# Longer waits ahead of layer 1's table and state products, C matrices on POOL's queue, readout products in one burst

## The chip, the cores and the metric

The kernel runs on one core of one Trainium2 chip. The metric is the device time of one execution in microseconds (us). The names of the engines are those of the profile: PE is the tensor engine, PEld its weight loads, DVE the vector engine, ACT the scalar engine, POOL GpSimd, SP the engine that issues most of the DMAs.

## The reference

Two layers, 256 latent and 256 context tokens of width 1024. Layer 0 treats all 512 tokens, layer 1 only the latent ones (of the context it needs the S5 states alone).

```python
for l in range(DEPTH):
    ...
    hc = _modulate(xc, g_norm1[l], csh1, csc1)
    if l == DEPTH - 1:
        ctx_states = _s5_states(hc @ w_in[l][:, :W_BRANCH], *s5p, None)
    else:
        zc = hc @ w_in[l]
        ctx_states = _s5_states(zc[..., :W_BRANCH], *s5p, None)
        xc = xc + cga1 * _token_mixer(zc, ctx_states, p)
        xc = xc + cga2 * _sq_relu_mlp(_modulate(xc, g_norm2[l], csh2, csc2), mlp_w1[l], mlp_w2[l])
    ctx_final = _s5_final(ctx_states)
    h = _modulate(x, g_norm1[l], sh1, sc1)
    z = h @ w_in[l]
    lat_states = _s5_states(z[..., :W_BRANCH], *s5p, ctx_final)
    x = x + ga1 * _token_mixer(z, lat_states, p)
    x = x + ga2 * _sq_relu_mlp(_modulate(x, g_norm2[l], sh2, sc2), mlp_w1[l], mlp_w2[l])
return _rms_norm(x, g_final)
```

`_token_mixer` runs four branches (the S5 scan in two directions, a Fourier mixing, pooling, a convolution module), gates each with a sigmoid of its own part of z, projects and adds them. The change touches the S5 branch only: 16 groups of 16 channels, 64 complex states for each group and direction, h_t = a h_(t-1) + Bbar u_t, and y = Re(C h) + D u.

## The kernel before

All large products are float32, done as three products of two-part operands (`mm3`): a 128x128 tile of weights costs three matmuls, on 512 columns in layer 0 and 256 in layer 1. Below they are called main products. `Stream` brings the weights in blocks of 512 KB by SP's queue; ACT makes the high part of each and DVE the low part (tiles called `parts`).

One program writes all instructions out ahead of time. It walks through the main products, and after every three of them calls `pump()`, which may let background tasks write some of theirs in between. A task is a generator: `yield "w", x` holds it back until x us more of the tensor engine's modelled time have been written. So the order on each engine is fixed by these numbers; on the chip an engine works through its instructions in that order and waits at one whose input is late.

The S5 branch works on chunks of 8 tokens, so that only 32 chunk states are scanned for each half of the tokens. Its steps, all background tasks:

- `tables_b` makes the powers of a times Bbar, eight pieces: some arithmetic, four transposes on PE, a copy, a DMA to a scratch in DRAM (`scr_b`).
- `tables_c` makes C times the powers of a, eight pieces (u, k): it loads the C matrices of each u (`load`, from the input `in_s5c`), fills `BL` with zeros (the MEMSET) and then with Bbar (the TENSOR_SCALAR), multiplies C with the powers, multiplies `BL` with the result on PE (`products`, four products of 112 columns, for k=1 eight more), and stores the result (`scr_c`).
- In layer 0 these arithmetic steps have two buffers (nb = 2). Layer 1's tables are made on POOL beside layer 0's MLP, with one buffer of each kind (nb = 1): a piece's arithmetic can start only when the stores of the piece before it have left the buffer.
- `states` loads the S5 input by chunks from a scratch (`load_u`: `scan<-scr_z`, on POOL's queue) and multiplies it with the B tables: four groups of 16 products of 64 columns.
- `scan` runs on DVE and POOL.
- `readout` makes y: for each unit (h, g) eight products of the window `T` and then four groups of eight products of the states with the C tables, all into the same two PSUM banks, 128 columns each. Layer 0 has four units, layer 1 two. In the trace eight such products are 16 records, since float32 goes through PE twice.

Every operation goes through `Engine.call`, so in the trace nearly every line is L64.

Of the kernel before, what the change touches and what calls it, by code (L numbers as in the profile page):

```python
# [25 lines left out]
class Alloc:  # L26
    """A bump allocator over one SBUF region (words of a partition)."""
# [24 lines left out]
class Engine:  # L52
    """An engine that keeps a clock of what it has been given, against the tensor engine's."""
# [15 lines left out]
class Engines:  # L69
    """The engines of a core, each with its clock."""  # L70
# [34 lines left out]
class S5:  # L105
    """The bidirectional state-space scan, in chunks of 8 tokens.

    Tokens: 64 chunks (32 of the context, 32 of the latents), seg = stream.
    State rows: partition (gi, p) for group g = 2 q + gi, free (direction k, q).
    """  # L110
# [135 lines left out]
    def powers(self, E, base, W, plan):  # L246
        """base[.., d:d+n] = base[.., s:s+n] * base[.., m]."""
        na = base.shape[2]
        for d, s, m, n in plan:
            t1 = W[:, 0:2 * na * n].rearrange("p (r a i) -> p r a i", r=2, i=n)  # L250
            sh = [128, na, n]
            br = bc(base[:, 0, :, m:m + 1], sh)
            bi = bc(base[:, 1, :, m:m + 1], sh)
            o = base[:, :, :, d:d + n]
            x = base[:, :, :, s:s + n]
            E.tensor_tensor(t1[:, 0], x[:, 1], bi, op=MUL)
            E.tensor_tensor(t1[:, 1], x[:, 0], bi, op=MUL)
            E.tensor_tensor(o[:, 0], x[:, 0], br, op=MUL)
            E.tensor_tensor(o[:, 1], x[:, 1], br, op=MUL)
            E.tensor_tensor(o[:, 0], o[:, 0], t1[:, 0], op=SUB)  # L260
            E.tensor_tensor(o[:, 1], o[:, 1], t1[:, 1], op=ADD)
            yield

# [1 line left out]
    def tables_b(self, A, E):  # L265
        K, l = self.K, self.l
        nc = K.nc
# [16 lines left out]
        for i in range(8):  # L284
# [14 lines left out]
            if nb == 1:  # L299
                yield "w", 6.0  # L300
            if i >= nb - 1:
                products(i + 1 - nb)
            if nb == 1:
                yield "w", 4.0
# [6 lines left out]
    def tables_c(self, A, E):  # L311
# [12 lines left out]
        def load(u):  # L324
            nc.sync.dma_start(CCs[u % 2], K.I["s5c"][l][u])
# [38 lines left out]
        for u in range(4):  # L364
# [8 lines left out]
            for k in range(2):  # L373
# [13 lines left out]
                if nb == 1:  # L387
                    yield "w", 6.0
# [3 lines left out]
                if nb == 1:  # L392
                    yield "w", 4.0
# [7 lines left out]
    def store_u(self, t, ps):  # L401
        """ps: the projection of channel tile t, [128, 512 tokens] in PSUM."""
        K = self.K
        z = K.tmp()
        K.nc.scalar.activation(
            z.rearrange("p (s j) -> p j s", s=8), ps.rearrange("p (j s) -> p j s", s=8), AF.Copy)
        K.nc.scalar.dma_start(K.Z[self.l][t], z)
# [20 lines left out]
    def permute(self, i, raw, T):  # L428
        """The windows of the kernel with their columns in the order of the readout."""
        self.K.nc.scalar.activation(T[:, 1024 * i:1024 * i + 1024].rearrange("p (g c t) -> p g c t", g=8, c=16),  # L430
                                    raw[:, 1024 * i:1024 * i + 1024].rearrange("p (g t c) -> p g c t", g=8, c=16),
                                    AF.Copy)

# [7 lines left out]
    def begin(self):  # L441
        """Space, and the tables as far as there is space for them."""
# [14 lines left out]
    def states(self):  # L457
# [3 lines left out]
        yield "w", 5.87 + (0.0 if l else 2.0)  # L461
# [27 lines left out]
    def scan_tables(self, E):  # L489
        """Powers of a^8, for both parts of every state; in the place of bbar and rev."""  # L490
# [32 lines left out]
    def level(self, k, i, p0, step, n, g0=0):  # L523
        """Positions p0, p0 + step, .. += a^(8 2^i) times the one before by 2^i in the direction's order."""
# [25 lines left out]
    def scan(self):  # L550
        """The scan over chunks: sums over pairs, fours, eights, then over the eights in order, and back."""
# [18 lines left out]
        # over the groups of eight chunks, in the order of the scan  # L570
# [29 lines left out]
    def readout(self):  # L600
        """y: [channel, (half, stream, step, chunk)], in the place of the tables of the scan."""
# [12 lines left out]
        for h in range(2):  # L614
# [13 lines left out]
            for g in gs:  # L628
# [8 lines left out]
                yield "w", 1.5  # L637
                for j, (k, r) in enumerate(((0, 0), (0, 1), (1, 0), (1, 1))):
# [8 lines left out]
                    yield "w", 1.5  # L647
# [11 lines left out]
    def load_d(self):  # L659
        """The input of the scan by channels."""  # L660
# [4 lines left out]
class Stream:  # L665
    """The large weights, in the order of their use: loaded ahead, split into two float32r parts."""
# [10 lines left out]
    def lend(self, until, slots):  # L677
        """More space for the parts of the entries before one."""
# [50 lines left out]
    def release(self, key=None):  # L729
        """Gives back the space of an entry, or of the first that holds some."""  # L730
# [7 lines left out]
class Model:  # L738
# [55 lines left out]
    def pool(self, side, dtype=F32, **sizes):  # L794
        """Tiles on a side of the shared space, in the place of what was there."""
# [4 lines left out]
    def open_scan(self, l):  # L800
        """Space for the state-space branch (and in the first layer for the convolution)."""
# [6 lines left out]
    def open_parts(self, w):  # L808
        """The parts of the merged branches in the place of the last two branches' space."""
# [17 lines left out]
    def open_hidden(self, i, l):  # L827
        """Space for a half of the MLP's hidden features at a time."""
# [11 lines left out]
    def lend_y(self, l):  # L840
        """Space for weights that a mixer needs from its first branch's output on."""
# [14 lines left out]
    def hold(self, n):  # L856
        """Waits until n banks can be kept beyond a step and one is left."""
# [9 lines left out]
    def defer(self, f):  # L867
        """Work that waits for another engine, to be given to its own a little later."""
# [6 lines left out]
    def mm3(self, out, w, x, start, stop):  # L875
        """out += w^T x for w and x in two float32r parts."""
# [9 lines left out]
    def after(self, *cbs):  # L886
        """After the products of an output tile: what follows the tile before, the next weights, background."""
# [16 lines left out]
    def pump(self):  # L904
        """Background work, as long as its engines are not behind: a task's step yields nothing, a wait
        in the tensor engine's time, or the engines of its next steps."""
# [42 lines left out]
    def order(self, l):  # L949
        """The branches of a mixer: f the inputs of the Fourier branch, g a tile of gates, y a branch's  # L950
        output in two parts, q a tile of its projection; each with the branch and the tile."""
# [36 lines left out]
    def warm(self, n):  # L988
        """Products that keep the tensor engine's clock up while the first data comes; nothing reads them."""
# [9 lines left out]
    def mod_part(self):  # L999
        """Two of the eight row tiles of four column tiles of the first norm's modulation, both conditions."""  # L1000
# [13 lines left out]
    def mod_finish(self, m):  # L1014
        """Shift and scale of two tiles of features."""
# [10 lines left out]
    def mod_bias(self, l, m, c, raw):  # L1026
        """Four column tiles of the modulation from their products, and what the norms need of them."""
# [11 lines left out]
    def mods(self):  # L1039
        """The modulation's other column tiles, with the rows of the weights on the free axis."""  # L1040
# [39 lines left out]
    def mod_need(self, l, m):  # L1080
        """The modulation's column tiles before one."""
# [47 lines left out]
    def norm_sums(self, acc, n, width):  # L1129
        """1 / sqrt(column sums of acc / width + eps) as diagonal matrices of tokens."""  # L1130
# [10 lines left out]
    def norm_bcast(self, d, n):  # L1141
        """The diagonal on every partition, in PSUM."""
# [7 lines left out]
    def h_tiles(self, l, which, r, c0, n):  # L1150
        """h = x r g (1 + scale) + shift in two parts; yields the tiles of features, one product ahead."""
# [49 lines left out]
    def turn(self, l, part, keys, xh, xl, l2, which, order):  # L1201
        """The last four output tiles before a norm; the norm of one half runs beside the products of the other."""
# [49 lines left out]
    def turned(self, h, l2, which, order, group):  # L1252
        """The first group of products after the norm, for one half; the norm and h of the other."""
# [32 lines left out]
    def layer(self, l):  # L1286
# [5 lines left out]
        # first output tiles, by rows of the weights as h comes  # L1292
# [196 lines left out]
        # output projection  # L1489
# [19 lines left out]
        # MLP  # L1509
# [127 lines left out]
    def shift_columns(self):  # L1637
        """The second norm's shift as columns before those of the tokens, which go without it and the norm's factor."""
# [35 lines left out]
    def run(self):  # L1674
# [61 lines left out]
        # the last norm, on the way to rows of tokens  # L1736
# [28 lines left out]
class Branches:  # L1765
    """The pooling, Fourier and convolution branches of a layer; y: their output in float32."""
# [12 lines left out]
    def linear(self, w, x):  # L1779
        """w^T x for a [256, 256] matrix and x [128, 2 n]; yields the two tiles in PSUM."""  # L1780
# [8 lines left out]
    # pooling  # L1789
# [52 lines left out]
    # Fourier mixing  # L1842
# [36 lines left out]
    # convolution  # L1879
# [20 lines left out]
    def conv(self):  # L1900
# [12 lines left out]
        # layer norm over the channels  # L1913
# [45 lines left out]
class S5L:  # L1959
    """The state-space branch of a layer."""  # L1960
# [105 lines left out]
def _rows(a):  # L2066
    """[.., 128 k] vectors onto partitions: [.., 128, k]."""
# [70 lines left out]
```

## Time and profile before

| | |
|---|---|
| time, median of 3 runs | 1219.62 us (1215.27 to 1221.63) |
| span of the profiled execution | 1223.4 us |
| PE busy | 1169.3 us, 96% of the span |
| DVE busy | 977.2 us, 80% |
| ACT busy | 515.9 us, 42% |
| POOL busy | 277.2 us, 23% |
| moved by DMA | 211.49 MB |

The profile is of one execution; its span lies 0.3% above the median, and what lies around the span is not shown. A row of the timeline gives the start, the length, the engine, the line, the operation with the tile it writes and those it reads, the count, and in brackets the idle time ahead of it with what ended it.

### The profile page before, as it was taken

To read this page: it belongs to the slowest core of one execution; us is meant where nothing else is said; L and a number is where in the kernel's file an instruction comes from. 1 tells how busy PE (TensorE), PEld (TensorE's weight loads), DVE (VectorE), ACT (ScalarE), POOL (GpSimd) and SP (SyncE) were. 2 spreads that over 40 slices of the span, in tenths; PEclk is the share of its full clock that TensorE was granted. 3 is DMA by queue.
4 is the path that set the end of the run, shared out by engine and by line. 5 is a ranking of instruction groups with operands and counts; after the bars stand their busy time and mean duration, and the time that the engine had idled before them with its cause. 6 is when DMAs were issued, how large, how long until landed. Compare 5 with 4: busy or idle time off the path is not lost.

```text
span 1223.4 us, 20288 instructions
## 1 busy us (share of the span) xinstructions
PE 1169.3 (96%) x7770; PEld 1007.1 (82%) x7770; DVE 977.2 (80%) x1878; ACT 515.9 (42%) x872; POOL 277.2 (23%) x315
## 2 busy tenths in 40 slices
PE   7999996999999999999988989998999999999997
PEld 5777775776787988888876878897999999999997
DVE  6789999788799769999986884556898788867664
ACT  4534342333334465422421433335544455645443
POOL 0048754000000100176535462030530002000000
PEclk9999998999999999999998999999999999999999
DMA  9543522546464514466676765335444445555551
GB/s 375 216 134 125 167 84 94 181 163 203 134 209 161 180 34 149 138 194 219 198 254 230 267 212 206 121 121 160 168 159 163 162 155 198 186 186 189 179 186 52
DMA packets 66961, 211.49 MB, mean 173 GB/s; under 512 B 7984, under 2 KB 14128, under 8 KB 66864
## 3 DMA queue, kind: packets, MB, share of 16 engines
q1 hardware_dynamic: 56032, 184.10, 44.8%
q10 hardware_dynamic: 7696, 14.56, 3.2%
q0 software_dynamic: 3136, 11.54, 2.9%
q8 instruction: 61, 1.00, 0.3%
q14 instruction: 36, 0.29, 0.1%
HBM read 199.19 MB, written 10.98 MB: 172 GB/s over the span
## 4 chain that ended last, share of the span: by engine, by line
PE 55%; DVE 26%; issue 6%; DMA 5%; ACT 4%; POOL 3%; ACTq 0%; DVEq 0%; POOLq 0%; SPq 0%
PE bank L64 55%; DVE whole L64 9%; DVE parts L64 7%; DVE scan L64 5%; DVE mixer L64 2%; ACT parts L64 2%; DMA whole<-in_w_modt_dram 1%; ACT whole L64 1%; POOL whole L64 1%; POOL tables L64 1%; DMA scr_c<-tables 1%; DVE windows L64 1%; DMA whole<-in_w_dram 1%; POOL scan L64 1%; DMA whole<-in_w_br_dram 1%
## 5 line engine op out<-in xcount | busy, mean ns | idle before, releaser
L64 PE MATMUL bank<-parts 128*128 128x512 f32 (+2 forms) x4008 | 729.2, 339 | 17.7 <-DVE parts L64 14.5
L64 PEld LDWEIGHTS bank<-parts 128*128 128x128 f32 x4008 | 612.4, 190 | 107.5 <-DVE parts L64 20.2
L64 ACT ACTIVATE parts<-whole 128x1024 fp32r<-128x1024 f32 (+1 forms) x288 | 273.1, 959 | 150.7 <-PE bank L64 67.7
L64 DVE TENSOR_TENSOR parts<-whole,parts 128x1024 fp32r<-128x1024 f32 (+1 forms) x240 | 292.7, 1227 | 16.4 <-ACT parts L64 16.0
L64 PE MATMUL bank<-hidden,parts 128*128 128x256 f32 (+1 forms) x1440 | 253.9, 337 | 0.0
L64 PEld LDWEIGHTS bank<-hidden,parts 128*128 128x128 f32 x1440 | 219.6, 190 | 30.6 <-issue 0.5
L64 DVE SCALAR_TENSOR_TENSOR whole<-whole 128x1024 f32<-128x1024 f32 (+3 forms) x186 | 174.0, 937 | 18.8 <-DMA whole<-in_w_modt_dram 15.6
L64 POOL TENSOR_TENSOR whole<-whole 128x256 f32<-128x256 f32 (+1 forms) x69 | 53.2, 785 | 338.1 <-ACT whole L64 325.0
L64 DVE SCALAR_TENSOR_TENSOR whole<-bank,whole 128x256 f32<-128x256 f32 (+1 forms) x121 | 54.6, 475 | 67.5 <-PE bank L64 67.4
L64 ACT ACTIVATE whole<-whole 128x256 f32<-128x256 f32 (+2 forms) x139 | 48.7, 387 | 104.2 <-DVE whole L64 95.3
L64 ACT ACTIVATE whole<-bank 128x512 f32<-128x512 f32 (+2 forms) x69 | 35.5, 537 | 133.0 <-PE bank L64 92.6
L64 DVE TENSOR_TENSOR whole<-whole 128x256 f32<-128x256 f32 (+7 forms) x158 | 72.5, 464 | 18.8 <-ACT whole L64 16.4
L64 ACT ACTIVATE mixer<-bank 128x512 f32<-128x512 f32 (+1 forms) x84 | 40.7, 496 | 105.4 <-PE bank L64 99.2
L64 POOL TENSOR_TENSOR tables<-tables,whole 128x256 f32<-128x256 f32 x48 | 61.7, 1292 | 42.9 <-DMA scr_c<-tables 40.4
L64 DVE TENSOR_TENSOR hidden<-whole,hidden 128x512 fp32r<-128x512 f32 (+2 forms) x77 | 54.3, 709 | 9.4 <-ACT hidden L64 2.3
L64 ACT ACTIVATE hidden<-whole 128x512 fp32r<-128x512 f32 (+2 forms) x77 | 47.1, 615 | 8.1 <-PE bank L64 2.3
L64 ACT ACTIVATE tables<-bank 128x512 f32<-128x512 f32 (+2 forms) x20 | 8.4, 420 | 92.0 <-PE bank L64 91.7
L64 DVE SCALAR_TENSOR_TENSOR scan<-scan,whole 128x512 f32<-128x512 f32 (+1 forms) x64 | 47.0, 795 | 0.0
L64 POOL COPY whole<-whole 128x32 f32<-128x32 f32 x20 | 11.3, 599 | 150.0 <-DVE whole L64 150.0
L64 POOL TENSOR_TENSOR scan<-scan,whole 128x256 f32<-128x256 f32 (+3 forms) x50 | 41.3, 839 | 17.6 <-DVE scan L64 13.1
L64 DVE TENSOR_TENSOR scan<-scan,whole 128x256 f32<-128x256 f32 (+5 forms) x61 | 30.8, 531 | 13.4 <-ACT whole L64 12.5
L64 DVE TENSOR_TENSOR mixer<-bank,mixer 128x512 f32<-128x512 f32 (+1 forms) x56 | 31.6, 570 | 10.4 <-PE bank L64 9.8
(114 smaller groups left out, 904.9 us busy)
## 6 DMA issues: line engine op xcount, KB each, us to landing
whole<-in_w_dram SPq DMA_DIRECT2D x128, 512.0 KB, 4.3
whole<-in_w_in_dram SPq DMA_DIRECT2D x84, 512.0 KB, 4.2
whole<-in_w_modt_dram SPq DMA_DIRECT2D x77, 512.0 KB, 4.3
whole<-in_w_br_dram SPq DMA_DIRECT2D x16, 512.0 KB, 3.9
whole<-in_w_out_dram SPq DMA_DIRECT2D x16, 512.0 KB, 3.9
mixer<-in_w_mod_dram SPq DMA_DIRECT2D x8, 512.0 KB, 8.6
scan<-scr_b POOLq DMA_DIRECT2D x8, 512.0 KB, 5.7
scan<-in_w_mod_dram SPq DMA_DIRECT2D x6, 512.0 KB, 8.9
```

The costliest lines, as they stand in the source:

```text
L64: return f(out, *a, **k)
```

## The change

Five places. In layer 1's tables (nb == 1) the wait between a piece's arithmetic and its products grows from 6.0 to 8.0 us and the one behind the products shrinks from 4.0 to 2.0. Layer 1's C matrices are loaded by POOL's queue instead of SP's. The wait ahead of the state products grows from 5.87 to 10.5 us in layer 1 and from 7.87 to 8.5 in layer 0. In `readout` the waits between the five groups of a unit go, and one wait stays behind the last group. All docstrings and comments are removed too, which shifts line numbers by one (2137 lines become 2136).

```diff
@@ tables_b @@
             if nb == 1:
-                yield "w", 6.0
+                yield "w", 8.0
             if i >= nb - 1:
                 products(i + 1 - nb)
             if nb == 1:
-                yield "w", 4.0
+                yield "w", 2.0
@@ tables_c @@
         def load(u):
-            nc.sync.dma_start(CCs[u % 2], K.I["s5c"][l][u])
+            (nc.gpsimd if l else nc.sync).dma_start(CCs[u % 2], K.I["s5c"][l][u])
...
                 if nb == 1:
-                    yield "w", 6.0
+                    yield "w", 8.0
                 todo.append((u, k))
                 if len(todo) == nb:
                     products(*todo.pop(0))
                 if nb == 1:
-                    yield "w", 4.0
+                    yield "w", 2.0
@@ states @@
         self.load_u()
-        yield "w", 5.87 + (0.0 if l else 2.0)
+        yield "w", 10.5 if l else 8.5
@@ readout @@
-                yield "w", 1.5
                 for j, (k, r) in enumerate(((0, 0), (0, 1), (1, 0), (1, 1))):
                     for qq in range(4):
...
                             nc.tensor.matmul(py[gi][32 * qq:32 * qq + 32, 0:128],
                                              SB[k][ps, r, 4 * h + qq, g, k:k + 32], ca[ps, c:c + 128],
                                              start=False, stop=j == 3, tile_position=(64 * gi, 32 * qq))
-                    yield "w", 1.5
+                yield "w", 1.5
```

PE, the first product of layer 1's C tables (`tables 32x112`), which stands among layer 0's second MLP product (`hidden,parts`), before:

```order
L64 MATMUL bank_64<-hidden_3352,parts 128x512 x24
L64 MATMUL bank_65<-hidden_3352,parts 128x512 x24
L64 MATMUL bank_66<-hidden_3352,parts 128x512 x3
L64 MATMUL bank_68<-tables 32x112 x4
L64 MATMUL bank_66<-hidden_3352,parts 128x512 x21
L64 MATMUL bank_70<-hidden_3352,parts 128x512 x24
L64 MATMUL bank_63<-hidden_3352,parts 128x512 x6
L64 MATMUL bank_69<-tables 32x112 x4
```

and of the change:

```order
L64 MATMUL bank_64<-hidden_3352,parts 128x512 x24
L64 MATMUL bank_65<-hidden_3352,parts 128x512 x24
L64 MATMUL bank_66<-hidden_3352,parts 128x512 x12
L64 MATMUL bank_68<-tables 32x112 x4
L64 MATMUL bank_66<-hidden_3352,parts 128x512 x12
L64 MATMUL bank_70<-hidden_3352,parts 128x512 x24
L64 MATMUL bank_63<-hidden_3352,parts 128x512 x15
L64 MATMUL bank_69<-tables 32x112 x4
```

The product stands nine main products later; the 51 main products between one piece's products and the next are the same number as before.

POOL, the start of layer 1's C tables, before:

```order
L64 MEMSET tables 128x256
L64 TENSOR_SCALAR tables<-tables 128x64
L64 TENSOR_TENSOR tables<-tables,whole 128x256
L64 TENSOR_TENSOR whole<-tables,whole 128x256
L64 TENSOR_TENSOR tables<-tables,whole 128x256 x2
```

and of the change:

```order
L64 MEMSET tables 128x256
L64 DMA tables<-in_s5c_dram 128x128 x2
L64 TENSOR_SCALAR tables<-tables 128x64
L64 TENSOR_TENSOR tables<-tables,whole 128x256
L64 TENSOR_TENSOR whole<-tables,whole 128x256
```

The loads of the first two C matrices now stand in POOL's own order, right behind the MEMSET; each of the other two stands behind a piece with k=1 and ahead of the next TENSOR_SCALAR. Before, the four stood on SP among the weight loads.

PE, layer 1's state products (`scan 64x64`) among the input projection (`parts 128x256`), before:

```order
L64 MATMUL bank_66<-parts 128x256 x24
L64 MATMUL bank_70<-parts 128x256 x21
L64 MATMUL bank_68<-scan 64x64 x16
L64 MATMUL bank_70<-parts 128x256 x3
L64 MATMUL bank_63<-parts 128x256 x9
L64 MATMUL bank_69<-scan 64x64 x16
```

and of the change:

```order
L64 MATMUL bank_66<-parts 128x256 x24
L64 MATMUL bank_70<-parts 128x256 x24
L64 MATMUL bank_63<-parts 128x256 x24
L64 MATMUL bank_64<-parts 128x256 x15
L64 MATMUL bank_68<-scan 64x64 x16
L64 MATMUL bank_64<-parts 128x256 x3
```

The first group stands 42 main products later (3 + 24 + 15), and with it everything of the branch that follows.

## Rows read from the trace of the kernel before

**Rows 1.** The page, busy time of each engine, share of the span.

```profile
PE 1169.3 (96%) x7770; PEld 1007.1 (82%) x7770; DVE 977.2 (80%) x1878; ACT 515.9 (42%) x872; POOL 277.2 (23%) x315
```

**Rows 2.** Waits of PE: us in total, times, longest.

```profile
PE bank L64 <- POOL tables L64: 10.3, 5, 4.4
...
PE bank L64 <- issue: 3.9, 1, 3.9
```

**Rows 3.** Timeline of PE, first unit of layer 0's readout.

```profile
230.76 0.45 PE L64 MATMUL bank<-scan 64*32 64x128 f32 x16
231.14 2.35 PE L64 MATMUL bank<-parts 128*128 128x512 f32 x9
233.42 0.45 PE L64 MATMUL bank<-scan 64*32 64x128 f32 x16
```

**Rows 4.** Timeline of PE, main products behind a unit, then what follows.

```profile
311.37 19.36 PE L64 MATMUL bank<-parts 128*128 128x512 f32 x84
330.56 1.02 PE L64 MATMUL bank<-scan,whole 128*128 128x512 f32 x2
```

**Rows 5.** Timeline of PE cut off at 230.85: the first eight records alone.

```profile
230.76 0.34 PE L64 MATMUL bank<-scan 64*32 64x128 f32 x8
```

**Rows 6.** Timeline of PE, products of layer 1's C tables.

```profile
643.31 0.59 PE L64 MATMUL bank<-tables 128*32 128x112 f32 x4 [4.37 <-POOL tables L64]
646.17 0.59 PE L64 MATMUL bank<-tables 128*32 128x112 f32 x4 [2.28 <-POOL tables L64]
646.69 13.34 PE L64 MATMUL bank<-hidden,parts 128*128 128x512 f32 x51
...
726.31 0.39 PE L64 MATMUL bank<-tables 128*32 128x112 f32 x4 [1.69 <-POOL tables L64]
```

**Rows 7.** Timeline of POOL, layer 1's C tables.

```profile
624.66 0.31 POOL L64 MEMSET tables<- 128x256 f32 x1 [6.69 <-DMA scr_b<-tables]
638.38 1.04 POOL L64 TENSOR_SCALAR tables<-tables 128x64 f32<-128x64 f32 x1 [13.41 <-DMA tables<-in_s5c_dram]
...
644.53 1.59 POOL L64 TENSOR_TENSOR tables<-tables,whole 128x256 f32<-128x256 f32 x1
...
718.50 0.65 POOL L64 TENSOR_TENSOR tables<-tables,whole 128x256 f32<-128x256 f32 x1 [5.63 <-DMA scr_c<-tables]
```

**Rows 8.** Timeline of SP, the first two C loads.

```profile
633.40 0.86 SPq L325 DMA_DIRECT2D tables<-in_s5c_dram  x2
```

**Rows 9.** Loads from scr_z by POOL's queue, issue to landing.

```profile
DMA to landing us min/median/max: 4.1/5.4/7.9
```

**Rows 10.** Windows: us, busy PE, PEld, DVE, ACT, POOL, PEclk, DMA share, GB/s.

```profile
638.00:650.00 12.00, 5.35 (x22) 3.48 (x21) 10.97 (x16) 1.42 (x2) 7.58 (x7) 0.72 0.83 268
863.00:867.00 4.00, 4.00 (x75) 3.49 (x74) 2.82 (x8) 2.60 (x8) 0.53 (x1) 1.00 0.70 212
```

**Rows 11.** Timeline of PE, layer 1's state products.

```profile
846.11 5.42 PE L64 MATMUL bank<-parts 128*128 128x256 f32 x43 [0.49 <-DVE parts L64]
855.39 1.97 PE L64 MATMUL bank<-scan 128*64 128x64 f32 x32 [3.86 <-issue]
857.29 2.93 PE L64 MATMUL bank<-parts 128*128 128x256 f32 x12
860.15 1.49 PE L64 MATMUL bank<-scan 128*64 128x64 f32 x32
```

**Rows 12.** Timeline of POOL, layer 1's load of the S5 input.

```profile
847.26 1.18 POOL L64 DMA_DIRECT2D scan<-scr_z  x1 [27.38 <-DMA scr_z<-whole]
```

**Rows 13.** A window of layer 1, the columns of rows 10.

```profile
857.00:914.00 57.00, 55.08 (x481) 52.67 (x477) 53.09 (x131) 30.13 (x59) 28.36 (x35) 0.97 0.47 158
```

**Rows 14.** Timeline of PE, three waits on DVE and POOL.

```profile
208.85 1.65 PE L64 MATMUL bank<-parts 128*128 128x512 f32 x3 [9.53 <-DVE parts L64]
...
421.33 0.61 PE L64 MATMUL bank<-whole 128*128 128x1 f32 x4 [1.19 <-POOL whole L64]
...
914.02 0.38 PE L64 MATMUL bank<-parts 128*128 128x256 f32 x1 [1.11 <-DVE parts L64]
```

## The prediction, made before the changed kernel ran

> **What bounds the kernel now.** I read the page first. PE is busy 96% of the span and DVE 80% [rows 1], so nearly every microsecond has to come from PE: either it waits less, or it loses less between instructions, or it runs at its full clock for longer. So I next asked the view of waits what PE waits for. Of some 54 us idle, 10.3 us in five waits are for POOL's arithmetic on layer 1's tables, and one of 3.9 us is put down to "issue", which is a DMA here as shown below [rows 2]. Then I looked at the timeline of PE at each of the five places of the diff, and behind each at what comes next, since what PE no longer waits for here it may wait for there.
>
> **Readout bursts.** In the first unit of layer 0 a group of 16 records starts at 230.76, main products follow at 231.14, and the next group starts at 233.42 [rows 3]: 2.66 us for one group and nine main products. A main product costs (330.56 - 311.37) / 84 = 0.2285 us in a long run of them [rows 4], nine cost 2.06, so a group costs 0.60 us. How long would it take in a burst? The trace has no burst of several groups, but half a group shows the rate: the first eight records end at 230.76 + 0.34 = 231.10 [rows 5], all sixteen at 231.21 [rows 3], so eight more take 0.11 and sixteen 0.22. Each break of the main stream thus costs 0.60 - 0.22 = 0.38 us by itself. A unit breaks it five times before (the window's group and four others) and once after: 4 x 0.38 = 1.52 us, and 6 x 1.52 = 9.1 us for the six units. I take the same price for the 256-column products of layer 1. Lower bound: only the slow resumption of the main stream (0.60 less the 0.38 from 230.76 to 231.14, so 0.22) is saved, 6 x 4 x 0.22 = 5.3 us. The small products need no cover, since PE has none; what follows on ACT and DVE comes at nearly the same place, because the task waits 1.5 us behind the last group as before.
>
> The Trainium skill speaks against so short a group: by "TensorE: Matmul & The Clock Gate", section "Wait — 56ns, not 53.3ns?", matmuls start no closer than about 25 ns. Sixteen records would then take 0.40 us in a burst, and the bursts would save 4.8 us (an estimate from that page of the skill). The trace shows eight more records in 0.11 us, 14 ns each, which that rule does not allow, so the row decides.
>
> **Layer 1's tables.** PE reaches the first C product at 643.31 - 4.37 = 638.94, waits 4.37 us, and for its second half 2.28 more [rows 6]. What is late is POOL: it fills `BL` at 624.66, then idles 13.41 us for the C matrices until 638.38, and works until 644.53 + 1.59 = 646.12 [rows 7]. SP issues the two loads only at 633.40 [rows 8], between weight loads. From POOL's queue they can go out right behind the MEMSET. That one waits for the last B piece's store, whose product stands nine main products later now, 2.06 us, so the MEMSET ends at about 627.0. For the issue of two loads I take 1.2 us, that of the one in [rows 12], for the landing the median of POOL's loads from `scr_z`, 5.4 us [rows 9]: 633.6. POOL's work of 646.12 - 638.38 = 7.74 us ends at 641.4. PE comes nine main products later as well, at 641.0, so it waits 0.4 instead of 6.65: 6.25 us.
>
> With the wait goes a stretch at a lower clock. Between 638 and 650 the granted clock averages 0.72, a mixture of its two levels of 1.2 and 2.4 GHz, after PE was busy 5.35 of the 12 us [rows 10]; the 51 main products behind the wait take 13.34 us [rows 6] where 51 x 0.2285 = 11.65 would do. So 1.7 us more: 7.9 us in all. Lower bound: a landing of 7.9 us [rows 9] leaves 2.9 us of wait, and the low clock may stay: 6.65 - 2.9 = 3.7 us. The other waits for POOL's tables are 1.69 at 726.31 [rows 6] and 10.3 - 6.65 - 1.69 = 2.0. The loop behind them is products, store, POOL, products: POOL waits 5.63 us for the store [rows 7], and the store starts with the products. With 8.0 + 2.0 instead of 6.0 + 4.0 its period does not change, so I count nothing; upper bound both, 3.7 us, and the last 0.4.
>
> What is queued behind the moved loads? The third and fourth stand on POOL ahead of the next TENSOR_SCALAR, and wait there for a k=1 piece's products on PE, for which that instruction waits anyhow (one `BL`). They can cost their issue, at most 2 x 1.2 us, if POOL is the late one there; the pieces right behind them show no wait of PE, so I take nothing. SP loses a wait; no wait of PE is for a weight's DMA there, so this too is worth nothing.
>
> **State products.** In layer 1 the load of the S5 input is issued at 847.26 [rows 12], and PE waits from 851.53 until 855.39 [rows 11]: 8.1 us after the issue, so "issue" is this landing. A main product costs 5.42 / 43 = 0.126 us here, and 42 of them put PE's arrival at 856.8, after the landing: 3.86 us gained. The twelve main products behind the first two groups take 860.15 - 857.29 = 2.86 us [rows 11] where 1.51 would do, so 1.35 at the lower clock may come back: 5.2 us. But the branch now starts about as late as before in time and 42 products later in order, and DVE is busy 53.09 of the next 57 us [rows 13], with PE waiting 1.11 us for it at 914.02 [rows 14]. PE cannot arrive 5.2 us earlier at a DVE that has no room. I take half, 2.6 us, bounds 0 and 5.2. In layer 0 the step is 0.6 us, ahead of a wait of 9.53 us for DVE at 208.85 [rows 14] that takes up whatever is won or lost: nothing.
>
> **Given back.** What layer 0's bursts win is spent at the joins that depend on others. PE waits 1.19 us for POOL at 421.33 [rows 14]; it will wait longer there if it comes earlier. I take 1.5 us, bounds 0 and 4.
>
> **Sum.** 9.1 + 7.9 + 2.6 - 1.5 = 18.1 us. The profiled execution's 1223.4 would become 1205.3. It stands 3.8 us over the median of the runs, with what lies around the span unknown, so I take the difference off the median: 1219.6 - 18.1 = 1201.5, say 1202. A measurement tells about 0.5%, 6.1 us, from no change.
>
> **Rivals.**
> *DVE keeps the time.* PE comes earlier, but DVE's and POOL's chains in both layers end as before. For it: DVE's 53.09 of 57. Against: behind 209 us and beside the MLP DVE is no bound, by its 80%. Then the bursts and the state products are worth nothing: 7.9 us, 1212.
>
> *The loads are no earlier.* The C matrices land late on POOL's queue and each of the later ones delays POOL by its issue. For it: the landing reaches 7.9 us [rows 9]. Then tables give 3.7 - 2.4 = 1.3 us and the sum is 11.5, 1208. A rule of the Trainium skill stands beside it ("SBUF — State Buffer", "Who interferes with whom"): a DMA from POOL's queue can be starved while DVE holds the shared port in a two-port mode. DVE is busy 10.97 of 12 us there [rows 10], which would bear on it; the landings of 4.1 to 7.9 us already hold what such starving did to loads of that queue.
>
> *Both*, 1.3 - 1.5 or about no gain: 1220.
>
> *The clock falls at each burst.* Eighty small records in a row could be what a stretch of lower clock follows; each such stretch of 12 us at 0.72 costs 12 x 0.28 = 3.4 us [rows 10], six of them 20.2 us against the gain of 18.1: 1222, slower. It decides from 3.0 us a burst on. Against: from 863 to 867 PE runs 75 records in 4 us, most of them small ones of the state products, at a clock of 1.00 [rows 10].
>
> **How the numbers follow.** Forecast 0.56; DVE keeps the time 0.13; loads no earlier 0.10; both 0.10; clock at the bursts 0.08; better than the range 0.03. The forecast's own range goes from 9.1 + 12.0 + 5.2 - 0 = 26.3 us (1193) to a gain of 12 us (1208), since not all lower bounds meet. The range takes in the first two rivals, 0.79: 1193 to 1212. Faster by over 0.5% is the forecast, the first two rivals and the better case, 0.82. Of "both" 0.08 are within 0.5% and 0.02 slower, and the clock's 0.08 divide evenly: same 0.12, slower 0.06.
>
> **What would show it.** Each unit of the readout one run of 80 records of about 1.5 us, with no main products inside. The first C product without a wait above 1 us, POOL's wait for `in_s5c` at some 6 us instead of 13.41, and the 51 main products behind it in about 11.7 us. No wait for "issue" at layer 1's states, and the main products between the groups at 0.126 us. The forecast is wrong if PE's waits for DVE after layer 1's states, or at the joins of layer 0, grow by what was won, or if a burst is followed by rows of clock below 1.

## The result and the profile after

The changed kernel takes 1208.28 us (median of 4 runs, 1206.27 to 1211.11), the kernel before 1219.34 beside it. The ratio is 0.9897 with a 95% interval of 0.9862 to 0.9933: 12.6 us faster (8.2 to 16.8). The forecast was 18.1 us and 1202, with a range of 1193 to 1212. A second measurement gave 0.9871 (0.9839 to 0.9903).

The page of the changed kernel, busy time, against [rows 1]:

```profile
span 1207.2 us, 20297 instructions
...
PE 1160.9 (96%) x7770; PEld 1009.4 (84%) x7770; DVE 976.1 (81%) x1878; ACT 517.1 (43%) x872; POOL 282.9 (23%) x319
```

PE has the same 7770 instructions and is busy 8.4 us less; the stages below show where. Its waits:

```profile
PE bank L64 <- DVE parts L64: 16.6, 10, 7.8
...
PE bank L64 <- POOL tables L64: 4.2, 3, 3.0
```

The waits for POOL's tables went from 10.3 us to 4.2, and the one of 3.9 for "issue" [rows 2] is gone. The largest item, before as after, is DVE's low parts of the weights: 14.5 us before, 16.6 now.

The first readout units, timeline of PE, against [rows 3]:

```profile
228.94 1.75 PE L64 MATMUL bank<-scan 128*32 128x128 f32 x80
230.62 4.39 PE L64 MATMUL bank<-parts 128*128 128x512 f32 x18
```

Eighty records start at 228.94 and main products follow 1.68 us later, with no main product in between. Before, a unit's five groups had 36 main products between them. The eighty are of two kinds, sixteen of the window's products (128 rows) and sixty-four of the states' (64 rows); first the window's in the kernel before, then both kinds in the changed one:

```profile
227.89 0.67 PE L64 MATMUL bank<-scan 128*32 128x128 f32 x16 [0.97 <-ACT scan L64]
```

```profile
228.94 0.67 PE L64 MATMUL bank<-scan 128*32 128x128 f32 x16
```

```profile
229.53 1.16 PE L64 MATMUL bank<-scan 64*32 64x128 f32 x64
```

The window's sixteen take 0.60 us from their start to that of the next product in both kernels (228.49 before, 229.53 after). The sixty-four of the states take 1.09 us in the burst, 0.27 for sixteen, where a group of sixteen cost 0.60 between main products.

The start of layer 1's C tables, timeline of POOL, against [rows 7]:

```profile
619.99 0.31 POOL L64 MEMSET tables<- 128x256 f32 x1 [8.92 <-DMA scr_b<-tables]
620.47 1.15 POOL L64 DMA_DIRECT2D tables<-in_s5c_dram  x2 [0.17 <-issue]
624.54 1.31 POOL L64 TENSOR_SCALAR tables<-tables 128x64 f32<-128x64 f32 x1 [2.92 <-DMA tables<-in_s5c_dram]
...
631.99 1.61 POOL L64 TENSOR_TENSOR tables<-tables,whole 128x256 f32<-128x256 f32 x1
```

and PE beside it, against [rows 6]:

```profile
633.84 0.58 PE L64 MATMUL bank<-tables 128*32 128x112 f32 x8
634.35 12.17 PE L64 MATMUL bank<-hidden,parts 128*128 128x512 f32 x51
```

POOL waits 2.92 us for the C matrices instead of 13.41 and is done at 633.60; PE arrives at 633.84, 0.24 us later, and waits for nothing. From 628 to 640 the granted clock is 1.00, where the stretch of [rows 10] had 0.72:

```profile
628.00:640.00 12.00, 12.00 (x58) 9.37 (x57) 10.92 (x16) 2.62 (x4) 5.85 (x6) 1.00 0.84 293
```

Layer 1's states, timeline of PE, against [rows 11]:

```profile
842.28 1.15 PE L64 MATMUL bank<-scan 128*64 128x64 f32 x32
...
846.21 1.69 PE L64 MATMUL bank<-parts 128*128 128x256 f32 x12
...
861.40 4.85 PE L64 MATMUL bank<-parts 128*128 128x256 f32 x21 [3.17 <-DVE parts L64]
```

The wait ahead of the state products is gone, twelve main products take 1.69 us instead of 2.93, and 19 us later PE waits 3.17 us for DVE, where the longest such wait of this stage was 1.11 us before [rows 14].

### The profile page after: what moved, and what is told of

Same layout as the page of the kernel before. It is cut to its first block, busy times and chain, and to the rows that moved or that the text cites. A ratio compares the mean times of both kernels' runs of the same rounds, so it can differ in the third digit from the quotient of the medians.

```text
span 1207.2 us, 20297 instructions
## 1 busy us (share of the span) xinstructions
PE 1160.9 (96%) x7770; PEld 1009.4 (84%) x7770; DVE 976.1 (81%) x1878; ACT 517.1 (43%) x872; POOL 282.9 (23%) x319
## 4 chain that ended last, share of the span: by engine, by line
PE 72%; DVE 15%; POOL 3%; DMA 3%; issue 3%; ACT 3%; ACTq 0%; POOLq 0%; DVEq 0%; SPq 0%
PE bank L64 72%; DVE scan L64 5%; DVE parts L64 4%; DVE mixer L64 2%; DVE whole L64 2%; ACT parts L64 2%; POOL tables L64 1%; POOL whole L64 1%; ACT whole L64 1%; DVE windows L64 1%; POOL scan L64 1%; DMA whole<-in_w_in_dram 1%; DMA whole<-in_x_dram 0%; DMA scan<-scr_z 0%; DMA scr_c<-tables 0%
## 5 line engine op out<-in xcount | busy, mean ns | idle before, releaser
L64 PE MATMUL bank<-parts 128*128 128x512 f32 (+2 forms) x4008 | 727.2, 339 | 19.0 <-DVE parts L64 16.6
L64 PE MATMUL bank<-hidden,parts 128*128 128x256 f32 (+1 forms) x1440 | 251.2, 335 | 0.0
L64 DVE SCALAR_TENSOR_TENSOR whole<-whole 128x1024 f32<-128x1024 f32 (+4 forms) x188 | 175.7, 936 | 15.2 <-DMA whole<-in_w_modt_dram 12.0
L64 POOL TENSOR_TENSOR whole<-whole 128x256 f32<-128x256 f32 (+1 forms) x69 | 50.3, 743 | 347.2 <-ACT whole L64 342.2
L64 POOL TENSOR_TENSOR scan<-scan,whole 128x256 f32<-128x256 f32 (+3 forms) x50 | 44.0, 892 | 12.0 <-DVE scan L64 8.3
L64 DVE SCALAR_TENSOR_TENSOR scan<-scan,whole 128x512 f32<-128x512 f32 (+1 forms) x64 | 42.7, 728 | 0.0
L64 PE MATMUL bank<-merged,parts 128*128 128x256 f32 (+1 forms) x240 | 38.0, 316 | 0.8 <-DVE merged L64 0.8
```

Source lines behind the costliest of these rows:

```text
L64: return f(out, *a, **k)
```

## The experiments

Each kernel was compared with the kernel before on its own chip, in five rounds. Since the kernel before varies by several us from run to run, the times alone separate the smaller effects badly. I therefore also took stages from each profile, between rows that all kernels have: A the first product of layer 0's readout, B the first 512-column `merged,parts` product, C the row of layer 1's input projection that waits 0.8 us for ACT's `whole`, D the first 256-column `merged,parts` product. A to B holds layer 0's readout, B to C layer 1's tables, C to D layer 1's mixer. Everything behind D took 218.5 to 220.4 us in all kernels. A stage is read from one profiled execution; in C to D, kernels whose PE order is the same there (e1, e5 and e12) differ by 2.7 us.

| kernel | ratio to before (95%) | A to B | B to C | C to D |
|---|---|---|---|---|
| before | | 154.4 | 457.1 | 164.9 |
| changed | 0.9897 (0.9862-0.9933) | 149.4 | 446.8 | 162.5 |
| changed, again (e9) | 0.9871 (0.9839-0.9903) | 149.3 | 446.3 | 162.7 |
| before + bursts (e1) | 0.9907 (0.9874-0.9940) | 148.8 | 456.0 | 160.7 |
| before + tables (e2) | 0.9940 (0.9918-0.9962) | 154.7 | 447.2 | 165.7 |
| before + layer 1's states (e3) | 1.0023 (1.0000-1.0046) | 154.9 | 459.4 | 167.2 |
| before + layer 0's states (e4) | 1.0017 (0.9991-1.0043) | 156.4 | 455.4 | 163.5 |
| changed, states back (e5) | 0.9858 (0.9835-0.9882) | 148.8 | 446.1 | 159.4 |
| changed, C loads on SP (e6) | 0.9928 (0.9902-0.9954) | 149.4 | 451.8 | 163.3 |
| changed, windows on POOL (e7) | 0.9854 (0.9827-0.9881) | 149.4 | 441.4 | 160.3 |
| e5 and e7 together (e8) | 0.9838 (0.9811-0.9865) | 148.8 | 444.6 | 160.0 |
| changed, layer 1 spread (e10) | 0.9899 (0.9867-0.9932) | 149.3 | 448.3 | 165.3 |
| changed, waits 6 and 4 (e11) | 0.9867 (0.9840-0.9894) | 149.3 | 447.6 | 162.6 |
| changed, layer 1's states back (e12) | 0.9853 (0.9821-0.9885) | 149.4 | 447.6 | 162.1 |

**e1, the bursts alone.**

```diff
-                yield "w", 1.5
                 for j, (k, r) in enumerate(((0, 0), (0, 1), (1, 0), (1, 1))):
...
-                    yield "w", 1.5
+                yield "w", 1.5
```

> The kernel before with the readout's bursts alone. By the prediction's sum, 9.1 us less 1.5 given back: about 7.6 us faster, spread 6.1 in layer 0 and 3.0 in layer 1. If a burst is worth its price only where PE is not tied to DVE afterwards, layer 1's two units give nearly nothing: 5 to 6 us in all. If DVE keeps the time in both layers: under 1.5 us. If the short groups are bound by a start-to-start floor of 25 ns: 4.8 us, and 80 records take 2.0 us or more. If the clock falls at the bursts: slower.

11.4 us faster (7.3 to 15.4). A to B is 5.6 us shorter and C to D 4.2. PE's waits for DVE's parts are 14.5 us as before, so DVE takes nothing back, and the burst is not slowed to 25 ns a record.

**e2, the tables alone.**

```diff
-                yield "w", 6.0
+                yield "w", 8.0
...
-                yield "w", 4.0
+                yield "w", 2.0
...
-            nc.sync.dma_start(CCs[u % 2], K.I["s5c"][l][u])
+            (nc.gpsimd if l else nc.sync).dma_start(CCs[u % 2], K.I["s5c"][l][u])
```

> The kernel before with the 8.0 and 2.0 us waits of layer 1's tables and the C loads on POOL's queue. By the prediction 7.9 us faster: waits of PE for POOL's tables fall from 10.3 to about 4 us and the half-clock stretch behind them goes. If the loads are no earlier on POOL's queue: 1.3 us.

7.3 us faster (4.6 to 10.0), with 3.3 us of PE's waits for POOL's tables left. B to C is 9.9 us shorter.

**e3 and e4, the longer waits ahead of the states, layer 1 and layer 0.**

```diff
-        yield "w", 5.87 + (0.0 if l else 2.0)
+        yield "w", 10.5 if l else 7.87
```

> The kernel before with 10.5 instead of 5.87 us ahead of layer 1's states alone. By the prediction 2.6 us faster, half of the wait and the clock stretch that go. If DVE, which gets its work as late as before, takes all of it back: within 1 us of the kernel before, with PE's waits for DVE behind the states longer by about 5 us.

```diff
-        yield "w", 5.87 + (0.0 if l else 2.0)
+        yield "w", 5.87 if l else 8.5
```

> The kernel before with 8.5 instead of 7.87 us ahead of layer 0's states alone. By the prediction nothing, under 0.5 us, since a wait of 9.5 us for DVE stands behind. If the 3 to 4 us by which the changed kernel's profile is late between 160 and 220 us come from this edit: 2 to 4 us slower.

In layer 1 it is no gain: 2.8 us slower, with the interval from 0 to 5.6, and C to D grows by 2.3 us. PE's waits for DVE's parts there grow from 2.4 to 7.8 us, as was expected if DVE takes the gain back. In layer 0 the interval includes no change (1.1 us faster to 5.3 slower), and the profile shows no loss: layer 0's states lie ahead of A, which comes at 231.26 in e4 and at 227.89 in the kernel before, 3.4 us later, but e4's first main product of layer 0 is already 4.7 us later (27.21 against 22.52), ahead of anything that the edit touches. The timeline of DVE in e3 shows the first of its work that waits for the projection, against the same one in the kernel before:

```profile
863.28 0.43 DVE L64 TENSOR_TENSOR mixer<-mixer,whole 128x256 f32<-128x256 f32 x1 [7.24 <-ACT whole L64]
```

```profile
857.28 0.43 DVE L64 TENSOR_TENSOR mixer<-mixer,whole 128x256 f32<-128x256 f32 x1 [5.29 <-ACT whole L64]
```

ACT is not slow there. Just ahead it waits for a block of weights, in e3 and in the kernel before:

```profile
861.92 1.06 ACT L64 ACTIVATE parts<-whole 128x1024 fp32r<-128x1024 f32 x1 [10.44 <-DMA whole<-in_w_in_dram]
```

```profile
855.92 1.06 ACT L64 ACTIVATE parts<-whole 128x1024 fp32r<-128x1024 f32 x1 [8.62 <-DMA whole<-in_w_in_dram]
```

What stands ahead of the block is on SP (the changed kernel), and ACT's wait there:

```profile
826.48 6.69 SPq L424 DMA_DIRECT2D windows<-scr_k  x8
833.26 0.54 SPq L684 DMA_DIRECT2D whole<-in_w_in_dram  x1
```

```profile
840.89 1.06 ACT L64 ACTIVATE parts<-whole 128x1024 fp32r<-128x1024 f32 x1 [8.19 <-DMA whole<-in_w_in_dram]
```

The eight window loads of layer 1's readout occupy the queue for 6.7 us ahead of it. From this came a new theory, for e5 to e8 to test: in C to D DVE is the pace, ACT and DVE begin when this block has landed, and PE's gain at the states cannot last.

**e5 and e6, the changed kernel with one part undone.** e5:

```diff
-        yield "w", 10.5 if l else 8.5
+        yield "w", 5.87 if l else 7.87
```

> The changed kernel with the waits ahead of the states as before (5.87 and 7.87 us). Measured on its own the longer wait in layer 1 cost 2.8 us (0 to 5.6) and the one in layer 0 2.1 us (-1 to 5.3). If that adds up, this kernel is 2 to 5 us faster than the changed one, about 1205 us where the changed one is 1208 to 1211 (ratio to the kernel before about 0.986). If the prediction's term holds once the other edits are in, it is 2.6 us slower than the changed one (ratio about 0.992).

0.9858, lower than the changed kernel's 0.9897 and 0.9871, but the intervals overlap; C to D is 159.4 us against 162.5 and 162.7. So nothing speaks for the prediction's gain. The 3 us in the profile cannot be put down to the longer wait, though: in C to D the granted clock averaged 1.00 in e5 and 0.98 in the changed kernel, where 0.02 of 162.5 us is 3.2 us. The clock did not fall at e5's wait for the load, though PE waited 2.65 us there; e12, with the same PE order and a wait of 3.45 us, is at 0.98 too. The rows stand in the next section. e6:

```diff
-            (nc.gpsimd if l else nc.sync).dma_start(CCs[u % 2], K.I["s5c"][l][u])
+            nc.sync.dma_start(CCs[u % 2], K.I["s5c"][l][u])
```

> The changed kernel with layer 1's C loads back on SP's queue, the 8.0 and 2.0 us waits kept. If the early loads are what the tables gained, the first C product waits again: the loads leave SP some 6 us later than POOL's, 5 us and the clock stretch come back, 5 to 7 us slower than the changed kernel. If the longer wait alone did it, no more than 1 us slower.

0.9928, 3.8 and 7.0 us slower than the two measurements of the changed kernel. B to C grows by 5.0 us, and the first C product waits in both halves:

```profile
636.52 0.39 PE L64 MATMUL bank<-tables 128*32 128x112 f32 x4 [1.62 <-POOL tables L64]
638.52 0.39 PE L64 MATMUL bank<-tables 128*32 128x112 f32 x4 [1.61 <-POOL tables L64]
```

```profile
620.71 0.31 POOL L64 MEMSET tables<- 128x256 f32 x1 [8.66 <-DMA scr_b<-tables]
632.43 1.06 POOL L64 TENSOR_SCALAR tables<-tables 128x64 f32<-128x64 f32 x1 [11.40 <-DMA tables<-in_s5c_dram]
```

POOL waits 11.40 us for the matrices again. PE's 3.2 us here against 6.65 in [rows 6] is what the longer wait gives by itself.

**e7 and e8, the window loads on POOL's queue**, in e7 with the states of the changed kernel, in e8 with those of the kernel before:

```diff
-            K.nc.sync.dma_start(Tv[s].rearrange("c (g x) -> c g x", g=n),
+            (K.nc.gpsimd if self.l else K.nc.sync).dma_start(Tv[s].rearrange("c (g x) -> c g x", g=n),
```

> The changed kernel with layer 1's eight window loads on POOL's queue too, where POOL only waits for the input's store. If the weight block behind these loads on SP's queue, for which ACT waits 8.2 us and behind it DVE 4.5 us, is what sets the end of layer 1's mixer, ACT's wait falls to under 3 us, DVE starts 3 to 4 us earlier and the kernel is 2 to 4 us faster than the changed one. If DVE is late for another reason, no difference, within 1 us.

> The changed kernel with the states' waits as before and the eight window loads on POOL's queue. If the two causes are separate, both gains add: 4 to 8 us faster than the changed kernel. If the state products' place matters only as long as ACT waits for the late weight block, this is like the kernel with the window loads alone, within 1.5 us; PE then waits for the input's load, which stands behind the eight loads on POOL, 3 us or more.

In e7 ACT no longer waits for the block; what it waits for there is DVE:

```profile
830.69 1.06 ACT L64 ACTIVATE parts<-whole 128x1024 fp32r<-128x1024 f32 x1 [2.58 <-DVE mixer L64]
```

C to D falls to 160.3 us with the long wait and is 160.0 with the short one, against 159.4 of e5 with the block late: in this stage the gains do not add. By the times they may: e8 lies 4.0 and 7.2 us under the two measurements of the changed kernel, within the 4 to 8 expected if both gains add. The times (0.9854 and 0.9838) are not separated from the changed kernel or from each other by their intervals, so the two cases stay open. e8's PE waits 2.43 us for the input's load, less than the 3 us expected.

How the block comes earlier is only in part the queue. On POOL the window loads also go out at another time, 19.5 us ahead of C instead of 1.3 us behind it:

```profile
800.57 2.80 POOL L64 DMA_DIRECT2D windows<-scr_k  x5
```

The block's issue moves by 1.4 us alone (8.1 us behind C in the changed kernel, 6.7 in e7), while its time from issue to landing is halved; the changed kernel, then e7:

```profile
DMA to landing us min/median/max: 7.5/7.5/7.5
```

```profile
DMA to landing us min/median/max: 3.8/3.8/3.8
```

So of the 5.1 us by which the block comes earlier, 3.7 are a shorter transfer, away from the window loads; what lengthened it in the changed kernel is not shown further. e7's B to C is 5 us shorter as well. PE's waits there are shorter in e7, among them one of 3.0 us for POOL's tables that the changed kernel's profile has and this one has not; the edit does not explain it, and so e7's time is no clean test of the block.

**e9 to e12, on one chip.** e9 is the changed kernel again.

> The changed kernel itself, as the yardstick for the other three on this chip: 0.986 to 0.993 of the kernel before.

e10 spreads layer 1's units:

```diff
+                if l:
+                    yield "w", 1.5
                 for j, (k, r) in enumerate(((0, 0), (0, 1), (1, 0), (1, 1))):
...
-                yield "w", 1.5
+                    if l:
+                        yield "w", 1.5
+                if l == 0:
+                    yield "w", 1.5
```

> The changed kernel with layer 1's two readout units in five groups again. By the prediction two units are worth 3.0 us, so about 3 us slower than the changed kernel. If DVE sets the end of layer 1's mixer, the same within 1 us.

C to D is 2.6 us longer than in e9; by the times 3.4 us slower, which their intervals do not separate from zero. e11 takes the tables' waits back to 6.0 and 4.0:

```diff
-                yield "w", 8.0
+                yield "w", 6.0
...
-                yield "w", 2.0
+                yield "w", 4.0
```

> The changed kernel with layer 1's tables at 6.0 and 4.0 us again, the C loads still on POOL's queue. If the early loads gave nearly all of the tables' gain, within 1.5 us of the changed kernel: PE then comes 2.05 us earlier to each product, and so does the MEMSET. If the longer wait gave half, 3 to 4 us slower, with four to five waits of PE for POOL's tables of 1 to 2 us each.

No difference: 0.9867 against 0.9871, B to C 1.3 us longer than in e9. With the loads early, the longer wait gives next to nothing. e12 takes back layer 1's states:

```diff
-        yield "w", 10.5 if l else 8.5
+        yield "w", 5.87 if l else 8.5
```

> The changed kernel with 5.87 us ahead of layer 1's states again, layer 0 left at 8.5. By the prediction's term 2.6 us slower than the changed kernel. If what PE gained there is given back to DVE with interest, 2 to 3 us faster, with a wait of PE for the input's load of 2 to 4 us at the states and shorter waits for DVE behind.

0.9853 against 0.9871, 2.2 us faster, C to D 162.1 against 162.7. The time is on the side of "given back" and against the forecast of 2.6 us slower, but not resolved. The wait at the states is back, and those for DVE are short:

```profile
843.96 1.97 PE L64 MATMUL bank<-scan 128*64 128x64 f32 x32 [3.45 <-issue]
...
874.92 1.10 PE L64 MATMUL bank<-parts 128*128 128x256 f32 x7 [0.83 <-DVE parts L64]
```

## Why the prediction was right, and where it was not

The range of 1193 to 1212 held, but the time alone would mislead. The forecast's own range ended at 1208, and 1208.28 is what the rival "the loads are no earlier" gave; the stated range took the measured time in because it covered the rivals. The profiles show another sum: that rival is wrong, two terms came out, and one gave nothing.

**Readout bursts, 9.1 us: right.** At the same wait ahead of layer 0's states, layer 0's 6.1 us came out as 5.6 to 6.1 in A to B (7.87 us: 154.4 to 154.9 us with groups, 148.8 with bursts) and 7.0 (8.5 us: 156.4 and 149.3 to 149.4; in e4 PE also waited 1.5 us in this stage). Layer 1's 3.0 us came out as 4.2 (e1, where the clock of C to D was also 0.99 against 0.98) and 2.6 (e10). The mechanism is the one forecast: the main stream is broken once per unit, not five times. The price of a record was somewhat low, because the prediction gave all five groups the rate of [rows 5]. Those rows are of the unit's second group, a group of the states. The window's sixteen take 0.60 us in the burst too, and the states' 17 ns each instead of 14, so a burst takes 1.68 us and not 1.5. The rule of about 25 ns from start to start ("TensorE: Matmul & The Clock Gate", section "Wait — 56ns, not 53.3ns?", in the Trainium skill) is still not met, since 80 would then take 2.0 us. The rival of a clock that falls at the bursts fell. Granted clock over layer 0's four bursts and over layer 1's two, the last value but two:

```profile
228.00:268.00 40.00, 40.00 (x462) 30.63 (x461) 30.53 (x62) 17.16 (x28) 1.44 (x2) 1.00 0.54 184
907.00:930.00 23.00, 23.00 (x322) 21.94 (x322) 21.27 (x45) 11.40 (x21) 0.00 (x0) 1.00 0.49 160
```

**Layer 1's tables, 7.9 us: right in size and cause.** 7.3 us alone (e2). The loads go out 0.17 us behind the MEMSET, as forecast, and POOL goes on 4.1 us after their issue, sooner than the 1.2 and 5.4 us I took; the four C loads have 3.6, 4.4 and 5.7 us as minimum, median and maximum to landing. All 6.65 us of the first wait went, not 6.25. The 51 main products behind it take 12.17 us instead of 13.34 at a clock of 1.00, so 1.2 us came back and not 1.7; 11.65 was too little. In the window in which the first two loads were under way DVE was busy 2.69 of 4.20 us, and they landed in time, so the rival of loads that are no earlier fell:

```profile
620.40:624.60 4.20, 4.20 (x19) 3.38 (x19) 2.69 (x6) 2.39 (x6) 1.21 (x3) 1.00 0.76 255
```

The early loads do it: the long wait without them is worth about half (e6), and with them next to nothing (e11).

**Given back, 1.5 us: wrong, but small.** PE's wait of 1.19 us for POOL [rows 14] did not grow. In the changed kernel the same product waits for nothing:

```profile
414.97 0.50 PE L64 MATMUL bank<-whole 128*128 128x1 f32 x4
```

**State products, 2.6 us: the step that failed.** "I take half, 2.6 us, bounds 0 and 5.2" gained nothing: e3 is 2.8 us slower, with an interval from 0 to 5.6 that leaves no room for the forecast. The first part was right. The wait of 3.86 us and its stretch of lower clock go, as e12 shows by having both again. I also saw that DVE had no room. What I had wrong is that half would be left. PE waits the same time a little later, for DVE. From C to D, before and in the changed kernel:

```profile
PE bank L64 <- DVE parts L64: 2.4, 3, 1.1
```

```profile
PE bank L64 <- DVE parts L64: 6.2, 4, 3.2
```

And the clock falls at that wait instead. The first stretch is that of the states in the kernel before, the second that of the wait for DVE in the changed one:

```profile
847.00:863.00 16.00, 12.14 (x126) 11.56 (x125) 10.58 (x25) 3.21 (x12) 2.28 (x3) 0.79 0.79 258
```

```profile
857.00:873.00 16.00, 12.83 (x79) 12.36 (x78) 15.96 (x23) 6.18 (x8) 15.12 (x15) 0.79 0.29 102
```

So the 5.2 us gained at the states were spent 19 us behind them, which is the prediction's own sign of being wrong. Over the whole of C to D, in the kernel before, the changed one, e12 and e5:

```profile
839.37:1004.22 164.85, 157.71 (x1431) 150.49 (x1432) 138.18 (x307) 80.00 (x144) 29.54 (x36) 0.98 0.54 174
```

```profile
825.15:987.65 162.50, 155.53 (x1430) 150.71 (x1431) 138.70 (x307) 79.15 (x143) 27.19 (x36) 0.98 0.54 176
```

```profile
828.36:990.46 162.10, 155.44 (x1430) 150.50 (x1431) 138.18 (x307) 79.33 (x144) 28.63 (x36) 0.98 0.54 177
```

```profile
824.32:983.74 159.42, 152.96 (x1431) 148.13 (x1432) 138.57 (x307) 79.23 (x144) 28.79 (x36) 1.00 0.54 180
```

PE idles 7.1 us before, 7.0 in the changed kernel, 6.7 in e12 and 6.5 in e5. The 2.7 us between e12 and e5 go with the clock.

Why PE meets DVE there: DVE's scan stands behind the state products in order. Its first instruction, timeline of DVE in the kernel before and in the changed one:

```profile
880.12 0.10 DVE L64 MEMSET scan<- 128x16 f32 x2
```

```profile
869.91 0.10 DVE L64 MEMSET scan<- 128x16 f32 x2
```

Counted from C (839.37 and 825.15), that is 40.8 us before and 44.8 after; e12 has 40.4. The scan comes 4 us later, since DVE does more of the convolution first (it is busy 30.5 us between C and the scan before, 38.3 after), and the readout with it. PE meanwhile uses up the weights' low parts faster than DVE makes them, and waits (3.17 us at 861.40).

Whether the longer wait costs something beyond its missing gain stays open. Among the kernels with bursts, C to D is 162.5 to 163.3 us with it (changed, e6, e9, e11) and 159.4 to 162.1 without (e1, e5, e12), which speaks for some 2 us; part of that is the clock, and no time is clear of zero. That the scan's delay makes such a loss is not shown either. In e7 the scan still comes at 41.0 us against 38.3 in e8, and the readout 8 us later behind C, yet their C to D are the same.

**The sum.** 18.1 us were forecast and 12.6 measured, 15.8 in the second measurement. With the measured terms it is 11.4 for the bursts, 7.3 for the tables and 2.8 and 2.1 slower at the states of layers 1 and 0, neither clear of zero: 13.8 us. The state products' step in layer 1, 2.6 forecast and 2.8 slower, is the largest single error, 5.4 us of the 5.5 by which the forecast was too high. That it makes up nearly all of it is chance: each of these times has an interval of some 3 to 4 us either way, and the errors of the other terms cancel within them.

## What to carry to other kernels

A wait that PE loses by working ahead is not yet a gain: look for the next place at which it meets an engine without room, here DVE, and count the wait there and its stretch of lower clock. A forecast of "half" needs a reason for the half. Small products between large ones can cost more for the breaks than for themselves, here 0.33 us and 0.27 for a group of the states; one burst was worth it where all their inputs were there. A load that an engine waits for was well issued from that engine's own queue here, since the engine stood idle anyhow. Before a stage's time is put down to an edit, compare its granted clock: it went with 2.7 us here between two kernels of the same order.

## What the runs showed of the hardware

- In a burst, sixty-four records of 64 rows take 1.09 us, 17 ns each, and sixteen of 128 rows 0.60 us, 37 ns each. A single group of sixteen of the first kind costs 0.60 us between main products.
- Eight window loads occupied SP's queue for 6.69 us; the weight block behind them took 7.5 us from issue to landing, 3.8 in e7 without them, and ACT waited 8.2 us for it.
- The length of a wait did not tell whether the clock would fall. At layer 1's states PE waited 2.65 us in e5 and the clock of C to D stayed at 1.00; it waited 2.43 us in e8, and the 16 us around it (837 to 853) were at 0.89.
- The kernel before took 1215.05 to 1228.38 us in 29 runs beside e1 to e4. Effects of 2 us are hardly seen in the times, and in a stage of one profile only after its clock has been compared.
